# Three mixed cells of eight in an up projection, with the convolution listed piece by piece over the following cells

## The chip, the cores and the metric

One core of one Trainium2 chip runs the whole program. The metric is device time in microseconds (us), median of several executions. TensorE (PE) multiplies, VectorE (DVE) and ScalarE (ACT) work element by element, GpSimd (POOL) does a few small things, and SyncE (SP) issues most of the DMAs. ACT issues DMAs too, from a queue of its own.

## The reference

One decoder layer over 256 tokens of width 2048, all in float32: a mixer (a state-space group beside sliding-window attention), an FFN with a short convolution, and a per-layer embedding with a gate. The change lies in the FFN and the start of the embedding:

```python
h = h + jnp.concatenate([y_ssm, y_att], axis=-1) @ w_out[i]
u = _rmsnorm(h, ffn_norm_g[i]) @ w_up[i]          # 2048 -> 2 x 5632
u = _causal_dwconv(u, ffn_conv_w[i], ffn_conv_b[i])   # 3 taps along the tokens
g_ff, u_ff = jnp.split(u, [D_FF], axis=-1)
h = h + (jax.nn.silu(g_ff) * u_ff) @ w_down[i]
gate = jax.nn.sigmoid(_rmsnorm(h, ple_norm_g[i]) @ w_ple_gate[i])
pe = _rmsnorm(p[i] @ w_ple_proj[i], ple_post_g[i])
h = h + gate * pe
```

## The kernel before, in words

**Products.** Each float32 operand is split into a high and a low part (`split`, L203 to L209): ACT casts the high part (L205), DVE subtracts it from the source to get the low part (L206). A product then is three matmuls, hi x hi, hi x lo and lo x hi. Weights come in pieces of 128 x 1024 (two blocks of 128 rows by 512 columns). `load_raw` (L211) loads a piece through SP's queue into one of seven raw buffers `w`, and `split_w` (L219) makes `wh` and `wl` in one of five buffers (four in one pool, every fifth turn one in the FFN's pool). A raw buffer is free when its split is done, a split one when its matmuls are.

**The order of the work.** PE's order is the order of the program (`manual_schedule`). The other engines' rows are put in an order by a scheduler, which goes by priorities and by when it expects operands to be there. Each engine takes its instructions strictly in that order, so an instruction that waits holds up all behind it.

**The up projection.** `up(c)` (L1013) makes the gate columns and the up columns of chunk c (512 of each, 11 chunks, here called pairs) for both blocks of 128 tokens, in eight banks of PSUM. The sum over the 2048 rows goes in eight cells (`kp`) of 256 rows. A plain cell (`cell_plain`, L980) is 8 products, 24 matmuls of 128 x 512, with two weight pieces. A mixed cell (`cell_mixed`, L957) uses Strassen's scheme in Winograd's form: from sums and differences of the left side's blocks (made once, in `left`) and of the weights it takes 7 products, 21 matmuls. For that DVE makes four differences of weights, in `ta` and `tb` (L962); split are the gate piece, `ta`, `tb` and half of the up piece (`vh`, `vl`). Cells 0 and 4 are mixed. After the last of them four sums are made from the banks (L1029 to L1033), and after the last cell four more (L1035). They go to the staging tiles c0 to c3, and they set the banks free for the next pair.

**Behind a pair.** `finish` (L996) turns a half of the columns so that tokens lie along the rows: a copy (L1000), a transposing DMA from SP (L1002) and a copy into `uc` (L1003). Then `conv_tile` (L304) takes ACT's scaling with bias (L307) and two DVE steps (L309) for each of four blocks. After both halves come SiLU (L1037), the product (L1039) and the split of the product into the gated tiles `gh`, `gl`. All of that is listed at the end of `up`.

**The down projection.** The pairs are grouped in segments of 2, 2, 2, 2, 2 and 1 (L1065 to L1085). After each pair of a segment, half of the previous segment's down projection runs, in products of 12 matmuls (`down`, L1056). The first segment has none before it, so pairs 1, 2 and 3 follow each other without a down projection; the first one comes after pair 3.

**The entry.** When the mixer's output projection ends, the sum of squares of h is finished (L431, `squares` and `finish_rstd`) and its root taken. The first pair then runs its plain cells first (1, 2, 3, 5, 6, 7) and 0 and 4 last, since its left side has yet to be made. `boundary(1)` (L1042) runs, ahead of the first cell, the embedding's products `embed(0)` to `embed(3)` (L891; 12 matmuls each, whose results DVE copies to c0 to c3 (L896) and ACT's queue stores to `pe_d` (L897)), and between them `norm` and `left` for chunks 0 and 1 of h; chunks 2 and 3 follow ahead of cells 2 and 5. `norm(n)` (L901) scales 512 columns of h into `cv0` or `cv1` (n = 0 on DVE, L908; else on ACT, L906), and `left(n)` (L924) transposes them on PE (L932) and splits them with the gains, or for a mixed cell makes the seven sums and splits those. The embedding's left side `ph`, `pl` is loaded into `uc` and split (L887 to L889) when the mixer has ended.

Of the kernel before, what the change touches and what calls it, by code (L numbers as in the profile page):

```python
# [66 lines left out]
def hybrid_layer(  # L67
# [811 lines left out]
    with tc.tile_pool(name="ffn", bufs=2, reuse_waits="tile") as fp:  # L879
# [68 lines left out]
        def run(acc, lhs, rhs, start, stop):  # L948
            (hi, lo), (wh, wl) = lhs, rhs
            PE.matmul(acc, lhsT=hi, rhs=wh, start=start, stop=False)  # L950
            PE.matmul(acc, lhsT=hi, rhs=wl, start=False, stop=False)  # L951
            PE.matmul(acc, lhsT=lo, rhs=wh, start=False, stop=stop)  # L952

# [3 lines left out]
        def cell_mixed(acc, kp, c, first, last, fresh):  # L957
# [3 lines left out]
            for o, x0, x1 in ((ta[:, 0], wu[:, 0], wg[:, 0]), (ta[:, 1], wu[:, 1], wu[:, 0]), (tb[:, 0], wu[:, 1], ta[:, 0]), (tb[:, 1], wg[:, 1], tb[:, 0])):  # L961
                V.tensor_tensor(out=o, in0=x0, in1=x1, op=ALU.subtract)  # L962
# [232 lines left out]
```

## Time and profile before

| | before |
|---|---|
| median of 3 runs | 1435.52 us (1435.28 to 1436.73) |
| profiled execution | 1435.36 us, span 1433.6 us, mean granted clock 0.995 |
| PE, DVE, ACT busy | 1414.3, 1110.3, 901.6 us |
| matmul instructions | 6461 |
| entry to the FFN (last matmul of the mixer to the first of a cell) | 603.1 to 623.0 us of the span |
| pairs 1, 2, 3 | about 623 to 761 us |
| first down projection's start to 1320 | PE without a gap |

A row of a timeline gives start, duration, engine, line, the tiles (out, then in), and in brackets the idle time ahead and what ended it. A row of waits gives the total, the number and the longest. Durations of neighbouring instructions on an engine overlap a little, so the pitch from start to start is read beside them.

### The profile page before, as it was taken

The numbers are of one execution on the slowest core, as the hardware profiler recorded it, in microseconds if no ns is written. First come the engines' busy times: TensorE is split into PE (matmuls) and PEld (weight loads), VectorE is DVE, ScalarE is ACT, GpSimd is POOL, SyncE is SP. The second block draws the span as 40 slices with busy tenths as digits, with TensorE's granted clock in tenths as the row PEclk, the third lists the DMA queues.
The fourth block names the chain that finished last, engine by engine and source line by source line (L and its number), as shares of the span: only waits on it lengthen the run. The fifth ranks groups of instructions, "written<-read, shape, count | busy, mean of one in ns | idle before, by whom it ended". The sixth has DMA issues, their size and how long they took to land.

```text
span 1433.6 us, 18135 instructions
## 1 busy us (share of the span) xinstructions
PE 1414.3 (99%) x6461; PEld 1156.6 (81%) x6461; DVE 1110.3 (77%) x1480; ACT 901.6 (63%) x1196; POOL 131.5 (9%) x114
## 2 busy tenths in 40 slices
PE   9999999999999999898999999999999999999998
PEld 7888888888787778686888888888888888888887
DVE  7678876776778888688898887878788787877764
ACT  6675555644677666565787575666757576665653
POOL 0002010018344522000000000000000000000000
PEclk9999999999999999999999999999999999999999
DMA  9656655548777778565678677686766777676672
GB/s 340 232 173 207 208 184 184 162 151 231 191 208 200 205 224 227 180 229 157 191 221 219 226 213 210 217 228 199 220 216 185 239 215 214 204 222 214 219 253 67
DMA packets 164907, 296.80 MB, mean 207 GB/s; under 512 B 93201, under 2 KB 96081, under 8 KB 164177
## 3 DMA queue, kind: packets, MB, share of 16 engines
q1 hardware_dynamic: 162800, 289.94, 67.7%
q10 hardware_dynamic: 2016, 5.72, 1.1%
q8 instruction: 50, 0.82, 0.2%
q14 instruction: 41, 0.33, 0.1%
HBM read 270.41 MB, written 4.23 MB: 192 GB/s over the span
## 4 chain that ended last, share of the span: by engine, by line
PE 64%; DVE 4%; ACT 1%; issue 1%; DMA 0%; POOL 0%; DVEq 0%; ACTq 0%
PE b L951 10%; PE b L950 10%; PE b L952 10%; PE b L241 8%; PE b L243 8%; PE b L242 8%; PE acc L241 3%; PE acc L242 3%; PE acc L243 3%; DVE wl L206 2%; PE tr L802 1%; ACT wh L205 0%; PE sc L761 0%; DMA w<-in_w_up_dram 0%; PE b L293 0%
## 5 line engine op out<-in xcount | busy, mean ns | idle before, releaser
L206 DVE TENSOR_TENSOR wl<-w,wh 128x1024 fp32r<-128x1024 f32 (+1 forms) x473 | 582.7, 1240 | 208.2 <-ACT wh L205 207.3
L205 ACT CAST wh<-w 128x1024 fp32r<-128x1024 f32 (+1 forms) x473 | 488.5, 1044 | 320.5 <-PE b L952 110.7
L950 PE MATMUL b<-wh,ah 128*128 128x512 f32 x484 | 189.6, 392 | 3.9 <-DVE c L1032 2.0
L951 PE MATMUL b<-wl,ah 128*128 128x512 f32 x484 | 188.9, 390 | 0.3 <-DVE wl L206 0.3
L952 PE MATMUL b<-wh,al 128*128 128x512 f32 x484 | 189.0, 390 | 0.0
L242 PE MATMUL acc<-wl,ah 128*128 128x512 f32 x448 | 176.9, 395 | 0.0
L241 PE MATMUL acc<-wh,ah 128*128 128x512 f32 x448 | 175.8, 395 | 0.0
L243 PE MATMUL acc<-wh,al 128*128 128x512 f32 x448 | 175.6, 392 | 0.0
L241 PE MATMUL b<-wh,gh 128*128 128x512 f32 x352 | 137.1, 390 | 0.0
L243 PE MATMUL b<-wh,gl 128*128 128x512 f32 x352 | 137.0, 389 | 0.0
L242 PE MATMUL b<-wl,gh 128*128 128x512 f32 x352 | 136.9, 389 | 0.0
L950 PEld LDWEIGHTS b<-wh,ah 128*128 128x128 f32 x484 | 91.3, 189 | 24.5 <-ACT wh L205 2.4
L951 PEld LDWEIGHTS b<-wl,ah 128*128 128x128 f32 x484 | 91.2, 189 | 19.5 <-DVE wl L206 0.7
L952 PEld LDWEIGHTS b<-wh,al 128*128 128x128 f32 x484 | 91.2, 188 | 19.0
L241 PE MATMUL acc<-wh,yh 128*128 128x512 f32 x256 | 101.2, 395 | 0.3 <-DVE h L417 0.3
L242 PE MATMUL acc<-wl,yh 128*128 128x512 f32 x256 | 99.8, 390 | 0.0
L243 PE MATMUL acc<-wh,yl 128*128 128x512 f32 x256 | 99.6, 390 | 0.0
L241 PEld LDWEIGHTS acc<-wh,ah 128*128 128x128 f32 x448 | 84.2, 188 | 18.9 <-issue 1.1
L242 PEld LDWEIGHTS acc<-wl,ah 128*128 128x128 f32 x448 | 84.2, 188 | 18.4 <-issue 1.1
L243 PEld LDWEIGHTS acc<-wh,al 128*128 128x128 f32 x448 | 84.2, 188 | 17.8 <-issue 0.7
L243 PEld LDWEIGHTS b<-wh,gl 128*128 128x128 f32 x352 | 66.1, 188 | 13.7
L242 PEld LDWEIGHTS b<-wl,gh 128*128 128x128 f32 x352 | 66.1, 188 | 13.7
(289 smaller groups left out, 2256.7 us busy)
## 6 DMA issues: line engine op xcount, KB each, us to landing
w<-in_w_up_dram SPq DMA_DIRECT2D x176, 512.0 KB, 4.4
w<-in_w_in_dram SPq DMA_DIRECT2D x126, 512.0 KB, 4.1
w<-in_w_down_dram SPq DMA_DIRECT2D x88, 512.0 KB, 4.3
w<-in_w_out_dram SPq DMA_DIRECT2D x64, 512.0 KB, 4.1
w<-in_w_pg_dram SPq DMA_DIRECT2D x32, 512.0 KB, 4.4
seg<-scr SPq DMA_DIRECT2D x8, 512.0 KB, 5.0
xt<-in_xT_dram SPq DMA_DIRECT2D x16, 128.0 KB, 6.9
h<-in_x_dram SPq DMA_DIRECT2D x2, 1024.0 KB, 7.7
```

The costliest lines, as they stand in the source:

```text
L205: S.copy(hi, src)
L206: V.tensor_tensor(out=lo, in0=src, in1=hi.bitcast(F32), op=ALU.subtract)
L241: PE.matmul(acc[b], lhsT=hi, rhs=wh[:, i, :], start=(k == 0), stop=False)
L242: PE.matmul(acc[b], lhsT=hi, rhs=wl[:, i, :], start=False, stop=False)
L243: PE.matmul(acc[b], lhsT=lo, rhs=wh[:, i, :], start=False, stop=(k == total - 1 or (b == NB - 1 and k + 1 == whole)))
L802: PE.matmul(v3(o[e * HD : (e + 1) * HD, kv * 2 * P : (kv + 1) * 2 * P], 2), lhsT=v[kb][:, vs], rhs=pT[e][:, :, kb, :], start=(kb == 0), st ...
L950: PE.matmul(acc, lhsT=hi, rhs=wh, start=start, stop=False)
L951: PE.matmul(acc, lhsT=hi, rhs=wl, start=False, stop=False)
L952: PE.matmul(acc, lhsT=lo, rhs=wh, start=False, stop=stop)
```

## The change

- `MIXED` becomes (0, 3, 5). The first pair's order of cells becomes 1, 2, 0, 4, 3, 6, 5, 7, and chunks 2 and 3 of `norm` and `left` both come ahead of cell 2. The left side of plain cells 1 and 2 now lies in `ah3` and `al3`.
- The embedding's left side is loaded and split in the attention part (`at[88]`), into parts of `ah3` and `al3`, and the convolution's weights `fcw` are loaded there too. `embed` stores through SP's queue instead of ACT's. The last sum of squares, its root, and `norm` and `left` of chunks 0 and 1 get high priority.
- `cell_mixed` makes `ta` after it has listed the split of the gate piece, and `tb` after the split of `ta`.
- The convolution of a pair is cut into eight pieces, with the product and its split as a ninth. They are listed over the following work: one after each mixed cell, two after each plain one, one after each piece of a down projection, and what is left at the end of the next pair. `uc` has two buffers instead of one, and the gated tiles have three.
- `Banks` counts the products of each bank, which sets the start and stop flags of the matmuls.

```diff
-MIXED = (0, 4)
+MIXED = (0, 3, 5)
...
+        def embedding():
+            pt_ = sb(act, [P, KG, T], "ah3")[:, :KW, :]
+            nc.scalar.dma_start(pt_, pT)
+            nc.scalar.dma_start(fcw, ffn_cw)
+            t = sb(act, [P, KG, T], "al3", F32R)
+            em.extend((t[:, :KW, :], t[:, KW:, :]))
+            split(pt_, *em)
+
+        at[88] = embedding
...
-        squares(ssh, 3)
-
-    rh = finish_rstd(ssh, "rh")
+        with tc.high_priority():
+            squares(ssh, 3)
+
+    with tc.high_priority():
+        rh = finish_rstd(ssh, "rh")
...
-        pt_ = sb(fp, [P, 4, T], "uc", bufs=1)[:, :2, :]
-        nc.scalar.dma_start(pt_, pT)
-        ph, pl = (sb(fp, [P, KW, T], f"p{e}0", F32R, 1) for e in "hl")
-        split(pt_, ph, pl)
+        ph, pl = em
...
-                nc.scalar.dma_start(pe_d[b, :, n * NC : (n + 1) * NC], t)
+                nc.sync.dma_start(pe_d[b, :, n * NC : (n + 1) * NC], t)
...
-            for o, x0, x1 in ((ta[:, 0], wu[:, 0], wg[:, 0]), (ta[:, 1], wu[:, 1], wu[:, 0]), (tb[:, 0], wu[:, 1], ta[:, 0]), (tb[:, 1], wg[:, 1], tb[:, 0])):
+
+            def less(o, x0, x1):
                 V.tensor_tensor(out=o, in0=x0, in1=x1, op=ALU.subtract)
+
             g = split_w(wg)
+            less(ta[:, 0], wu[:, 0], wg[:, 0])
+            less(ta[:, 1], wu[:, 1], wu[:, 0])
             v = [sb(fp, [P, NC], f"v{e}", F32R, 1) for e in "hl"]
             split(wu[:, 1], *v)
-            a, b = split_w(ta), split_w(tb)
+            a = split_w(ta)
+            less(tb[:, 0], wu[:, 1], ta[:, 0])
+            less(tb[:, 1], wg[:, 1], tb[:, 0])
+            b = split_w(tb)
...
+        later = []
+
+        def step(n=1):
+            for _ in range(min(n, len(later))):
+                later.pop(0)()
...
+            def mult():
+                V.tensor_tensor(out=cvs[0], in0=cvs[0], in1=cvs[1], op=ALU.mult)
+                split(cvs[0], hi, lo)
+
+            later.extend([lambda e=e, f=f: conv(e, f) for e in range(2) for f in range(4)] + [mult])
...
-                kps.sort(key=lambda kp: kp in MIXED)
+                kps = plain[:-len(MIXED)]
+                for m, p in zip(MIXED, plain[-len(MIXED):]):
+                    kps += [m, p]
...
+                step(1 if kp in MIXED else 2)
+            step(len(later))
             for t, m in ((c0, Q2), (x, Q4), (y, Q3), (z, Q22)):
                 V.tensor_tensor(out=t, in0=t, in1=acc[m], op=ALU.add)
-            cg = finish(c, (c0, x))
-            S.activation(out=cg, in_=cg, func=AF.Silu)
-            cu = finish(NPAIR + c, (y, z))
-            V.tensor_tensor(out=cg, in0=cg, in1=cu, op=ALU.mult)
-            return cg
+            gated(c, (c0, x), (y, z), hi, lo)
...
-            if kp == 1:
+            if kp == plain[0]:
+                with tc.high_priority():
+                    norm(0)
                 for n in range(3):
                     embed(n)
-                norm(0)
-                left(0)
-                norm(1)
+                with tc.high_priority():
+                    left(0)
+                    norm(1)
                 embed(3)
-                left(1)
-            elif kp in (2, 5):
-                n = 2 + kp // 5
-                norm(n)
-                left(n)
+                with tc.high_priority():
+                    left(1)
+            for n in range(2, KG):
+                if kp == plain[min(n, len(plain) - len(MIXED)) - 1]:
+                    norm(n)
+                    left(n)
...
-                gemm(acc, lhs, [w_down[i, n] for i in range(i0 * KG // KW, (i0 + ni) * KG // KW)])
+                for s in range(total):
+                    products(acc, lhs, load_w(w_down[i0 * KG // KW + s, n]), s * KW, KW, total * KW, s == total - 1)
+                    step()
```

The order of the rows on an engine shows what is moved. Before, on DVE at the entry, from the last two weight splits of the mixer's time to the first copies of the embedding (`s1` and `rs_t` belong to the root, `cv0` is the first normed chunk, `c0` and `c1` hold embeddings, `pl0` is the low part of the embedding's left side):

```order
L206 TENSOR_TENSOR wl_1160_5536<-w_1158_5533,wh_1159_5535 128x1024
L206 TENSOR_TENSOR wl_1169_5580<-w_1167_5577,wh_1168_5579 128x1024
L431 TENSOR_REDUCE s1_1105_5373<-ssh_507_2637 128x2
L206 TENSOR_TENSOR pl0_1116_5408<-uc_1114_5405,ph0_1115_5407 128x512
L198 TENSOR_SCALAR rs_t_1106_5375<-s1_1105_5373 128x2
L908 TENSOR_SCALAR cv0_1147_5498<-h0_1_83,rh_1107_5377 128x512
L908 TENSOR_SCALAR cv0_1147_5498<-h1_2_84,rh_1107_5377 128x512
L896 COPY c0_1131_5440<-b_1126_5420 128x512
L896 COPY c1_1132_5443<-b_1127_5421 128x512
```

Now, right behind the same two splits (`ta`, `tb`, `vl` and their `w` belong to the first mixed cell):

```order
L997 TENSOR_TENSOR ta_1193_5705<-w_1192_5703,w_1191_5701 128x512
L997 TENSOR_TENSOR ta_1193_5705<-w_1192_5703 128x512
L918 COPY c0_1128_5435<-b_1123_5415 128x512
L432 TENSOR_REDUCE s1_1108_5380<-ssh_508_2638 128x2
L207 TENSOR_TENSOR vl_1198_5714<-w_1192_5703,vh_1197_5713 128x512
L918 COPY c1_1129_5438<-b_1124_5416 128x512
L997 TENSOR_TENSOR tb_1194_5706<-w_1192_5703,ta_1193_5705 128x512
L207 TENSOR_TENSOR wl_1169_5595<-w_1167_5592,wh_1168_5594 128x1024
L918 COPY c2_1135_5461<-b_1130_5441 128x512
L199 TENSOR_SCALAR rs_t_1109_5382<-s1_1108_5380 128x2
L918 COPY c3_1136_5464<-b_1131_5442 128x512
L997 TENSOR_TENSOR tb_1194_5706<-w_1191_5701,tb_1194_5706 128x512
```

and then:

```order
L207 TENSOR_TENSOR wl_1187_5668<-w_1185_5665,wh_1186_5667 128x1024
L918 COPY c0_1142_5487<-b_1137_5467 128x512
L918 COPY c1_1143_5490<-b_1138_5468 128x512
L930 TENSOR_SCALAR cv0_1122_5412<-h0_1_83,rh_1110_5384 128x512
L930 TENSOR_SCALAR cv0_1122_5412<-h1_2_84,rh_1110_5384 128x512
```

The subtractions and the half split of mixed cell 0, all copies of the first three embeddings and two weight splits now stand ahead of `cv0`; the split of `pl0` is gone from here.

Before, on DVE from the first pair to the second (`c0` to `c3` take the sums out of the banks, `ta` and `tb` belong to the second pair's first mixed cell from the second `ta` on):

```order
L206 TENSOR_TENSOR wl_1275_6036<-tb_1267_6018,wh_1274_6035 128x1024
L1031 TENSOR_TENSOR c1_1241_5941<-c2_1242_5942,b_1121_5415 128x512
L1035 TENSOR_TENSOR c0_1240_5940<-c0_1240_5940,b_1122_5416 128x512
L206 TENSOR_TENSOR wl_1278_6063<-w_1276_6060,wh_1277_6062 128x1024
L206 TENSOR_TENSOR wl_1281_6081<-w_1279_6078,wh_1280_6080 128x1024
L1032 TENSOR_TENSOR c2_1242_5942<-c2_1242_5942,b_1120_5414 128x512
L1035 TENSOR_TENSOR c1_1241_5941<-c1_1241_5941,b_1124_5418 128x512
L206 TENSOR_TENSOR wl_1287_6117<-w_1285_6114,wh_1286_6116 128x1024
L1033 TENSOR_TENSOR c3_1243_5943<-c2_1242_5942,b_1121_5415 128x512
L962 TENSOR_TENSOR ta_1296_6172<-w_1295_6170,w_1294_6168 128x512
L962 TENSOR_TENSOR ta_1296_6172<-w_1295_6170 128x512
L1035 TENSOR_TENSOR c2_1242_5942<-c2_1242_5942,b_1123_5417 128x512
```

Now, at the same place:

```order
L1085 TENSOR_TENSOR c2_1241_5916<-c0_1239_5914,b_1115_5405 128x512
L207 TENSOR_TENSOR wl_1278_6012<-ta_1271_5999,wh_1277_6011 128x1024
L1086 TENSOR_TENSOR c1_1240_5915<-c2_1241_5916,b_1117_5407 128x512
L207 TENSOR_TENSOR wl_1280_6018<-tb_1272_6000,wh_1279_6017 128x1024
L1092 TENSOR_TENSOR c0_1239_5914<-c0_1239_5914,b_1118_5408 128x512
L997 TENSOR_TENSOR ta_1297_6136<-w_1296_6134,w_1295_6132 128x512
L997 TENSOR_TENSOR ta_1297_6136<-w_1296_6134 128x512
L1087 TENSOR_TENSOR c2_1241_5916<-c2_1241_5916,b_1116_5406 128x512
L207 TENSOR_TENSOR wl_1284_6049<-w_1282_6046,wh_1283_6048 128x1024
L1092 TENSOR_TENSOR c1_1240_5915<-c1_1240_5915,b_1120_5410 128x512
L997 TENSOR_TENSOR tb_1298_6137<-w_1296_6134,ta_1297_6136 128x512
L1088 TENSOR_TENSOR c3_1242_5917<-c2_1241_5916,b_1117_5407 128x512
```

Sums of the banks, splits of the first pair's last mixed cell and subtractions of the second pair's first one are interleaved. Before, the first pair ended with a mixed cell as well.

In a later pair, on DVE at its first mixed cell, before (`cv0` and `cv1` take the convolution of the pair ahead, `h0` and `h1` the down projection's sums):

```order
L309 SCALAR_TENSOR_TENSOR cv0_1649_7808<-uc_1644_7797,fcw_1108_5389,cv0_1649_7808 128x254
L206 TENSOR_TENSOR wl_1697_8020<-w_1692_8009,wh_1696_8019 128x1024
L206 TENSOR_TENSOR wl_1701_8028<-ta_1694_8013,wh_1700_8027 128x1024
L206 TENSOR_TENSOR wl_1703_8032<-tb_1695_8014,wh_1702_8031 128x1024
L309 SCALAR_TENSOR_TENSOR cv1_1655_7833<-uc_1650_7822,fcw_1108_5389,cv1_1655_7833 128x255 x2
L417 TENSOR_TENSOR h0_1_83<-h0_1_83,b_1670_7925 128x512
L309 SCALAR_TENSOR_TENSOR cv1_1655_7833<-uc_1650_7822,fcw_1108_5389,cv1_1655_7833 128x255
L309 SCALAR_TENSOR_TENSOR cv1_1655_7833<-uc_1650_7822,fcw_1108_5389,cv1_1655_7833 128x254
L309 SCALAR_TENSOR_TENSOR cv1_1655_7833<-uc_1650_7822,fcw_1108_5389,cv1_1655_7833 128x255
L309 SCALAR_TENSOR_TENSOR cv1_1655_7833<-uc_1650_7822,fcw_1108_5389,cv1_1655_7833 128x254
L417 TENSOR_TENSOR h1_2_84<-h1_2_84,b_1671_7926 128x512
```

Now:

```order
L310 SCALAR_TENSOR_TENSOR cv0_1808_8441<-uc_1793_8399,fcw_18_144,cv0_1808_8441 128x254
L207 TENSOR_TENSOR wl_1848_8617<-w_1843_8610,wh_1847_8616 128x1024
L207 TENSOR_TENSOR wl_1852_8627<-ta_1845_8614,wh_1851_8626 128x1024
L310 SCALAR_TENSOR_TENSOR cv1_1823_8531<-uc_1798_8410,fcw_18_144,cv1_1823_8531 128x255 x4
L997 TENSOR_TENSOR ta_1869_8736<-w_1868_8734,w_1867_8732 128x512
L997 TENSOR_TENSOR ta_1869_8736<-w_1868_8734 128x512
L310 SCALAR_TENSOR_TENSOR cv1_1823_8531<-uc_1798_8410,fcw_18_144,cv1_1823_8531 128x254 x3
L207 TENSOR_TENSOR wl_1854_8633<-tb_1846_8615,wh_1853_8632 128x1024
L310 SCALAR_TENSOR_TENSOR cv1_1823_8531<-uc_1798_8410,fcw_18_144,cv1_1823_8531 128x254
L207 TENSOR_TENSOR wl_1857_8663<-w_1855_8660,wh_1856_8662 128x1024
```

The split of `tb` stood right behind that of `ta`. Seven steps of the convolution and the next mixed cell's two subtractions have moved between them.

More of the change, by code (lines that the diff above doesn't have):

```diff
@@ L193, in hybrid_layer @@
     posi = sb(const, [P, NB], "posi", I32)
+    fcw = sb(const, [P, 88 * 4], "fcw")
     fill(mc)
@@ L946, in left, with __init__, __getitem__, run @@
                 left_parts[kp] = hi, lo
[L948 to L952, printed above, removed]
         P1, P6, P7, P5, Q2, Q4, Q3, Q22 = range(8)
         A11, A12, A22, S1, S2, S3, S4 = range(7)
-        def cell_mixed(acc, kp, c, first, last, fresh):
+        class Banks:
+            def __init__(self):
+                self.t = [bank() for _ in range(8)]
+                self.left = [len(MIXED)] * 4 + [len(MIXED) + KW * len(plain)] * 3 + [KW * len(plain)]
+                self.used = set()
+            def __getitem__(self, m):
+                return self.t[m]
+            def run(self, m, lhs, rhs):
+                (hi, lo), (wh, wl) = lhs, rhs
+                self.left[m] -= 1
+                PE.matmul(self.t[m], lhsT=hi, rhs=wh, start=m not in self.used, stop=False)
+                PE.matmul(self.t[m], lhsT=hi, rhs=wl, start=False, stop=False)
+                PE.matmul(self.t[m], lhsT=lo, rhs=wh, start=False, stop=not self.left[m])
+                self.used.add(m)
+        def cell_mixed(acc, kp, c):
             wg, wu = (load_raw(w_up[n, kp]) for n in (c, NPAIR + c))
             ta, tb = (sb(fp, [P, KW, NC], t, bufs=1) for t in ("ta", "tb"))
-            for o, x0, x1 in ((ta[:, 0], wu[:, 0], wg[:, 0]), (ta[:, 1], wu[:, 1], wu[:, 0]), (tb[:, 0], wu[:, 1], ta[:, 0]), (tb[:, 1], wg[:, 1], tb[:, 0])):
+            def less(o, x0, x1):
                 V.tensor_tensor(out=o, in0=x0, in1=x1, op=ALU.subtract)
             g = split_w(wg)
+            less(ta[:, 0], wu[:, 0], wg[:, 0])
+            less(ta[:, 1], wu[:, 1], wu[:, 0])
             v = [sb(fp, [P, NC], f"v{e}", F32R, 1) for e in "hl"]
             split(wu[:, 1], *v)
-            a, b = split_w(ta), split_w(tb)
+            a = split_w(ta)
+            less(tb[:, 0], wu[:, 1], ta[:, 0])
+            less(tb[:, 1], wg[:, 1], tb[:, 0])
+            b = split_w(tb)
             right = {P1: (g, 0), Q2: (g, 1), P5: (a, 0), P7: (a, 1), P6: (b, 0), Q4: (b, 1)}
@@ L969, in cell_mixed @@
             left_ = {P1: A11, Q2: A12, Q3: S4, P5: S1, P7: S3, P6: S2, Q4: A22}
-            order = (P1, P5, P7, P6, Q4, Q2, Q3) if first and fresh else (P1, Q2, Q3, P5, P7, P6, Q4)
+            order = (P1, Q2, Q3, P5, P7, P6, Q4) if acc.used else (P1, P5, P7, P6, Q4, Q2, Q3)
             for m in order:
@@ L977, in cell_mixed, with cell_plain @@
                     r = [t[:, i, :] for t in w]
-                run(acc[m], (hi[:, f, :], lo[:, f, :]), r, first and (fresh or m in (P1, P5, P6, P7)), last and (m in (P1, P5, P6, P7) or not fresh))
-        def cell_plain(acc, kp, c, first, last, fresh):
+                acc.run(m, (hi[:, f, :], lo[:, f, :]), r)
+        def cell_plain(acc, kp, c):
             h, l = left_parts[kp]
@@ L987, in cell_plain, with turned @@
                         bs = slice(b * P, (b + 1) * P)
-                        run(
-                            acc[m],
-                            (h[:, i, bs], l[:, i, bs]),
-                            [t[:, i, :] for t in w],
-                            first and (not fresh or m == Q22) and i == 0,
-                            last and (fresh or m == Q22) and i == KW - 1,
-                        )
-        def finish(c, us):
-            uc = sb(fp, [P, 4, T], "uc", bufs=1)
+                        acc.run(m, (h[:, i, bs], l[:, i, bs]), [t[:, i, :] for t in w])
+        later = []
+        def step(n=1):
+            for _ in range(min(n, len(later))):
+                later.pop(0)()
+        def turned(us):
+            uc = sb(fp, [P, 4, T], "uc")
             for b in range(NB):
@@ L1077, in hybrid_layer @@
             pair += np_
+        step(len(later))
         h2T = Lhs(act, KT, "a")
```

55 lines of the change are left out of this document (32 added, 23 removed).

## Prediction

> **What bounds the kernel now.** I read the page first, for the busy shares:
>
> ```profile
> span 1433.6 us, 18135 instructions
> PE 1414.3 (99%) x6461; PEld 1156.6 (81%) x6461; DVE 1110.3 (77%) x1480; ACT 901.6 (63%) x1196; POOL 131.5 (9%) x114
> ```
>
> TensorE (PE) has work 99% of the span, so what counts is the number of its matmuls, and the few places where it waits. Next came the view of PE's waits (line, releaser; total us, times, longest), of which these four lie in the part that the change touches:
>
> ```profile
> PE b L241 <- ACT ph L205: 4.1, 1, 4.1
> PE b L950 <- DVE c L1035: 2.8, 2, 1.4
> PE b L950 <- DVE c L1032: 2.0, 1, 2.0
> PE b L950 <- DVE c L1033: 0.5, 1, 0.5
> ```
>
> PE's timeline puts the first at the entry to the FFN: the last matmul of the mixer's output projection, the embedding's first and last half-speed ones, the transposes of the first normed chunk (called T(0) below), and the first up-projection matmul. The last five rows are the end of the first pair and the start of the second:
>
> ```profile
> 603.10 0.39 PE L243 MATMUL acc<-wh,yl 128*128 128x512 f32 x1
> 607.60 0.79 PE L241 MATMUL b<-wh,ph 128*128 128x512 f32 x1 [4.11 <-ACT ph L205]
> 612.15 0.63 PE L242 MATMUL b<-wl,ph 128*128 128x512 f32 x1
> 612.58 0.63 PE L243 MATMUL b<-wh,pl 128*128 128x512 f32 x1
> 618.58 1.04 PE L932 MATMUL b<-ident,cv 128*128 128x128 f32 x8
> 619.38 0.47 PE L241 MATMUL b<-wh,ph 128*128 128x512 f32 x1
> 623.02 0.48 PE L950 MATMUL b<-wh,ah 128*128 128x512 f32 x1
> 670.37 0.50 PE L950 MATMUL b<-wh,ah 128*128 128x512 f32 x1 [1.38 <-DVE c L1035]
> 673.33 0.47 PE L950 MATMUL b<-wh,ah 128*128 128x512 f32 x1 [1.98 <-DVE c L1032]
> 675.56 0.79 PE L950 MATMUL b<-wh,ah 128*128 128x512 f32 x1 [0.48 <-DVE c L1033]
> 678.65 0.80 PE L950 MATMUL b<-vh,ah 128*128 128x512 f32 x1 [1.44 <-DVE c L1035]
> 681.38 0.46 PE L950 MATMUL b<-wh,ah 128*128 128x512 f32 x1
> ```
>
> From 612.15 to 612.58 is 0.43 us for one matmul; elsewhere the pitch is about half of that. The windows give the pitch and the granted clock by stage (us, busy and count of each engine, clock, DMA):
>
> ```profile
> 603.50:623.00 19.50, 15.40 (x64) 12.38 (x65) 14.12 (x23) 11.35 (x19) 0.71 (x1) 0.82 0.69 217
> 667.50:682.00 14.50, 9.12 (x26) 5.54 (x26) 13.30 (x18) 9.92 (x11) 0.00 (x0) 0.76 0.89 237
> 641.20:761.10 119.90, 114.20 (x489) 92.21 (x488) 103.54 (x137) 84.56 (x99) 0.00 (x0) 0.97 0.68 200
> 846.80:889.10 42.30, 42.30 (x189) 35.02 (x188) 35.33 (x42) 23.07 (x25) 0.00 (x0) 1.00 0.67 211
> 724.50:1320.00 595.50, 595.50 (x2629) 493.23 (x2628) 487.69 (x619) 393.89 (x444) 0.00 (x0) 1.00 0.73 216
> ```
>
> The stretch from 846.80 is the up projection of one later pair: two mixed cells of 21 matmuls and six plain ones of 24, 186 (three of the 189 overlap the edges), in 42.30 us: 0.2275 us a matmul. From 724.5 on PE is busy in every microsecond and VectorE (DVE) in 487.69 of 595.50, 82%. So the steady part is bound by matmuls alone, and before it lie two losses. The entry: from 603.5 to 607.6 PE idles, and about 12 matmuls then run at 0.43, 7.0 us in all (4.1, and 12 x 0.20, and the slow first one). The first transitions: from 641.2 to 761.1 lie 486 matmuls, 110.6 us at 0.2275, in 119.9, so 9.4 us are lost, nearly all between 667.5 and 682, where DVE is busy 13.30 of 14.50.
>
> **The change part by part.** The sum is made against the profiled execution, 1435.36 us with a span of 1433.6; the median of the runs shown is 1435.52, 0.01% above it.
>
> *Matmuls.* A third mixed cell in each of 11 pairs takes away 24 - 21 = 3 matmuls: 33 x 0.2275 = **-7.5 us**. They lie in stretches where PE is never idle, so all of it counts unless DVE takes it back.
>
> The Trainium skill ("TensorE: Matmul & The Clock Gate", "Wait — 56ns, not 53.3ns?") states 215.7 ns from start to start for 512 columns at the warm clock; by that the term would be 7.1. The trace has 227.5, and the sum goes by it.
>
> *DVE's price.* By form, count, busy us and mean ns of one:
>
> ```profile
> L206 DVE TENSOR_TENSOR wl<-w,wh 128x1024 fp32r<-128x1024 f32 x467 | 578.6, 1247 | 205.7 <-ACT wh L205 204.8
> L962 DVE TENSOR_TENSOR tb<-w,ta 128x512 f32<-128x512 f32 x22 | 15.0, 684 | 0.0
> L206 DVE TENSOR_TENSOR vl<-w,vh 128x512 fp32r<-128x512 f32 x22 | 15.0, 684 | 0.0
> L309 DVE SCALAR_TENSOR_TENSOR cv<-uc,fcw,cv 128x254 f32<-128x254 f32 x88 | 40.8, 477 | 0.0
> L1035 DVE TENSOR_TENSOR c<-c,b 128x512 f32<-128x512 f32 x44 | 28.8, 680 | 0.0
> ```
>
> Back to back they overlap by some 0.08 us, as DVE's timeline shows at the second transition:
>
> ```profile
> 704.54 0.68 DVE L1030 TENSOR_TENSOR c<-c,b 128x512 f32<-128x512 f32 x1
> 705.14 1.22 DVE L206 TENSOR_TENSOR wl<-w,wh 128x1024 fp32r<-128x1024 f32 x1
> 706.28 0.68 DVE L962 TENSOR_TENSOR ta<-w,w 128x512 f32<-128x512 f32 x1
> ```
>
> So 0.60 for 512 columns, 1.13 for 1024, and 0.40 for a convolution step. A mixed cell costs DVE four subtractions, one half split and three whole ones: 5 x 0.60 + 3 x 1.13 = 6.4. A plain cell costs two splits, 2.26. A pair besides has eight sums out of the banks (4.8), 16 convolution steps (6.4), the product and its split (2.3): 13.5. That makes 2 x 6.4 + 6 x 2.26 + 13.5 = 39.8 per pair before, and 3 x 6.4 + 5 x 2.26 + 13.5 = 43.9 after. PE takes 42.3 before and 183 x 0.2275 = 41.6 after.
>
> *Steady pairs.* Eight pairs have a down projection with each up: 96 matmuls more for PE (21.8 us), eight splits and four additions for DVE (11.4). DVE then needs 55.4 of 63.5 us, 87%. Taken at **0**, covered by the weight buffers (four, and one more): PE holds up to five halves of a cell, 2.7 us each. Without that cover it costs rival B's price.
>
> *Entry.* The embedding's left side is loaded and split in the attention part, at slot 88, so the wait of 4.11 goes: embed(0) to (2) can start at 603.6 and their 36 matmuls end at 611.8. The cast and subtraction, 0.6 us each, move to where ACT and DVE have slack: nothing, at most 1 us. But T(0) needs the normed chunk cv0 from DVE. In the trace, before T(0), stand:
>
> ```profile
> 603.03 1.28 DVE L417 TENSOR_TENSOR h<-h,acc 128x512 f32<-128x512 f32 x2
> 605.49 2.36 DVE L206 TENSOR_TENSOR wl<-w,wh 128x1024 fp32r<-128x1024 f32 x2 [1.19 <-ACT wh L205]
> 609.42 0.89 DVE L908 TENSOR_SCALAR cv<-h,rh 128x512 f32<-128x512 f32 x2 [0.82 <-POOL rh L200]
> ```
>
> In the new order 15 rows stand between those two splits and the first cv0: four subtractions of the first mixed cell, its half split, six copies of embeddings (11 x 0.60), two whole splits (2.3), two small ones (0.2): 9.1 us. The splits end at about 606.6, though the mixed cell's weights, issued when a split at 603 has freed their buffer, may land up to a microsecond later:
>
> ```profile
> w<-in_w_up_dram SPq DMA_DIRECT2D x176, 512.0 KB, 4.4
> pe_d<-c ACTq DMA_DIRECT2D x8, 256.0 KB, 4.6
> ```
>
> cv0's first half is then ready at 616.2 to 617.1; I take T(0) at 616.4. PE has idled 4.6 us by then and, as after the 4.11 us at 607.6, runs at half speed for 5.4 us: T(0) 1.6, nine matmuls of embed(3) 3.8, three at full speed 0.7, T(1) 0.8, so the first plain cell starts at 623.3 instead of 623.02. Its low part lies in al3, which embed(3) reads until 622.5; behind that DVE has two copies, a split of 896 columns, a whole one and three pieces of gains, 4.5 us, up to the one that the cell's sixth matmul needs, at 626.8 where PE is there at 624.4. So 0.3 + 2.4 = **+2.7** against before (-4 if cv0 came in time, +5 if more of the queue is late).
>
> The same page ("Part 1: The HAM clock gate") states that the clock is halved after an idle window of about 3.4 us. The rows at 607.60 and after agree. By it the waits of 2 us below would cost no clock; but the rows at 675.56 and 678.65 are slow (0.63 to 0.80) after waits of 1.38, 1.98 and 0.48.
>
> *Stores of the embedding* go to SP's queue. Behind them wait weight loads, and the copies into c0 to c3 wait for the store two embeddings earlier. The first is issued at about 608.4 and lands by the 4.6 us above at 613.0, where the copy that needs it comes up at about 614.5: nothing, up to +1. ACT saves eight issues, which nothing waited for. fcw's earlier load, the third buffer of gated tiles and the second uc are priced at nothing, since no row names them as a releaser of PE.
>
> *Transitions without a down projection.* Pairs 2 and 3 follow without one, and there DVE needs 43.9 against PE's 41.6: a deficit of 2.3 each, 4.6 in all. DVE's own waits come on top (this row shows one):
>
> ```profile
> 676.71 0.69 DVE L962 TENSOR_TENSOR ta<-w,w 128x512 f32<-128x512 f32 x1 [1.20 <-DMA w<-in_w_up_dram]
> ```
>
> Two of these and some tenths: 2.7. With 1.0 for matmuls at half speed (five at 0.20) that is 8.3 instead of 9.4: **-1.1**. The mixed cell's splits in order of use help the first products of a cell; the convolution in pieces only spreads what DVE does.
>
> Sum: -7.5 + 2.7 + 0 - 1.1 = -5.9, so 1435.36 - 5.9 = **1429.5 us**.
>
> **The rivals.** *A, the stalls go as well.* If cv0 is in time (a subtraction that waits for its load being all that is late) and the spread convolution lets PE run through both transitions, the losses of 7.0 and 9.4 go with the matmuls: -23.9, 1411.5. For it: before, DVE was held up at 667.5 by convolution and bank sums in one lump, and ph was a plain mistake of order. Against: DVE's sums above, and 15 rows before cv0. Half of it gives 1418.
>
> *B, slower: the first mixed cell of each steady pair.* There the split of tb now stands behind seven convolution steps and two subtractions (2.8 + 1.2) and takes 1.1 itself, 5.1 us, while PE has six matmuls (1.4 us) between the first use of ta and that of tb. If DVE is less than 3.7 us ahead there, PE waits; 2.4 ahead costs 1.3 per pair, eight times: +10.4, in all -5.9 + 10.4 = +4.5, 1439.9. Against: five buffers let DVE run 5 to 8 us ahead, and in 595.5 us before PE never waited.
>
> *C, no change.* Entry and transitions eat it: a cold clock at both transitions, 12.0 us instead of 8.3, and 5 instead of 2.7 at the entry: 1429.5 + 3.7 + 2.3 = 1435.5. For it: the row of 13.30 busy of 14.50, where a third mixed cell leaves DVE no slack.
>
> That the change doesn't take place is excluded: PE's order has 33 rows fewer.
>
> **How the numbers follow.** The forecast has 0.55, A 0.17, B 0.10, C 0.15, the rest 0.03. A measurement of this kernel can tell about 0.2%, 2.9 us, from no change; the bounds are 1432.6 and 1438.4. The forecast's own spread (entry -4 to +5, transitions 2 either way) is 1424 to 1434. Faster: A, most of the forecast: 0.74. Within: C and the forecast's upper end: 0.16. Slower: 0.10. The range leaves out B and the lower half of A: 1416 to 1437.
>
> **What would show it.** Right: PE counts 33 fewer; a wait at T(0) of 4 to 5 us on cv from DVE where 4.11 on ph stood, then matmuls at 0.43; waits for DVE's sums (L1085 to L1092) or splits (L207) of some 8 us in the two transitions; none from about 720 on, and the steady up at 41.6. Wrong: T(0) without a wait (A), waits of L986's rows on wl from tb in each steady pair (B), or an up that isn't 0.7 us shorter.

## The result, and the profile after

The changed kernel takes 1445.03 us (median of 6 runs, 1440.78 to 1446.83), before 1436.45 (6 runs): ratio 1.0057, 95% interval 1.0041 to 1.0072. It is slower, where 1429.5 was forecast. The profiled execution took 1441.96 us (span 1440.2), 6.6 more than that of before, and is the second fastest of its six: the other 3 us up to the median have no profile, and what follows explains the 6.6.

PE's waits after:

```profile
PE b L954 <- DVE cv L930: 5.6, 1, 5.6
PE b L987 <- DVE wl L207: 4.8, 7, 1.4
PE b L986 <- DVE c L1092: 4.6, 3, 2.5
PE sc L762 <- POOL qT L713: 2.8, 2, 1.7
PE acc L242 <- DVE nm L774: 1.7, 1, 1.7
PE b L988 <- DVE al L210: 1.2, 1, 1.2
```

The wait for ph is gone, and one for cv0 stands in its place. The second row grew from one wait of 0.3 us before to seven. The fourth and fifth lie in the mixer, whose only term in the prediction, the moved cast and subtraction, was taken at nothing. The windows by stage, first of before (pairs 1 to 3, then the eight steady pairs), then of after (entry, pairs 1 to 3, steady pairs, and two single ups):

```profile
623.00:761.00 138.00, 132.30 (x577) 107.38 (x576) 119.77 (x163) 97.22 (x118) 0.00 (x0) 0.98 0.67 201
761.00:1272.40 511.40, 511.40 (x2258) 423.57 (x2257) 419.29 (x529) 335.37 (x377) 0.00 (x0) 1.00 0.72 214
```

```profile
607.60:627.40 19.80, 14.25 (x66) 11.62 (x64) 16.96 (x28) 11.19 (x18) 0.71 (x1) 0.91 0.83 271
627.40:765.70 138.30, 131.66 (x567) 106.29 (x566) 127.39 (x176) 100.55 (x123) 0.00 (x0) 0.98 0.61 189
765.70:1278.50 512.80, 508.79 (x2233) 418.10 (x2232) 453.77 (x580) 349.82 (x394) 0.00 (x0) 1.00 0.75 215
787.50:830.70 43.20, 41.80 (x185) 34.29 (x184) 39.10 (x46) 25.20 (x27) 0.00 (x0) 1.00 0.65 204
1044.80:1086.30 41.50, 41.50 (x185) 34.36 (x184) 37.37 (x42) 23.79 (x25) 0.00 (x0) 1.00 0.70 215
```

| stage | before | after | difference | forecast |
|---|---|---|---|---|
| up to the mixer's end | 603.5 | 607.6 | +4.1 | 0 |
| entry | 19.5 | 19.8 | +0.3 | +0.3 |
| pairs 1 to 3 | 138.0 | 138.3 | +0.3 | -0.7 (9 matmuls fewer -2.0, al3 +2.4, transitions -1.1) |
| eight steady pairs | 511.4 | 512.8 | +1.4 | -5.5 (24 matmuls fewer) |
| the rest | | | +0.5 | 0 |

Two of the eight ups of the steady pairs run in 41.5 us, as forecast; the others take 41.9 to 43.2, and what the eight have above 41.5 is 6.9 us in all. The first has most. The chain of waits there (start, us, what; `...` marks rows left out) shows why:

```profile
766.27 5.43 DMA flip<-half
...
772.80 0.99 ACT half L1041
...
776.85 5.29 DMA flip<-half
...
783.24 1.06 ACT wh L206
784.32 1.23 DVE wl L207
785.55 1.19 DVE cv L310 x3
786.73 1.20 DVE ta L997 x2
787.93 1.24 DVE cv L310 x4
789.18 0.25 issue
789.43 0.68 DVE h L418
790.11 1.15 DVE wl L207
791.30 0.50 PE b L987
```

Read upward from the last row: PE waits for the split of tb (790.11), which DVE reaches after a convolution of seven steps, two subtractions and a sum for h. All of these stand behind the split of ta (784.32), and that waits for ACT's cast of ta (783.24). On ACT the cast stands behind the copies of the turned columns, and those wait for two transposing DMAs of over 5 us, one after the other. PE's row says what it costs:

```profile
791.30 0.50 PE L987 MATMUL b<-wl,ah 128*128 128x512 f32 x1 [1.40 <-DVE wl L207]
```

PE's waits from 765.7 to 1278.5, all steady pairs together:

```profile
PE b L987 <- DVE wl L207: 4.0, 5, 1.4
```

The rest of the 6.9 are for the most part matmuls at and near such places that start 0.32 to 0.40 us apart instead of 0.23. Three of the five waits (1.40, 0.17 and 0.80) stand at the split of tb, as in the chain. The two others (0.82 and 0.79) come 11 to 12 us into their up, at the first split of its third cell, a plain one; first DVE's row, then PE's:

```profile
925.75 2.35 DVE L207 TENSOR_TENSOR wl<-w,wh 128x1024 fp32r<-128x1024 f32 x2
```

```profile
928.15 0.50 PE L987 MATMUL b<-wl,ah 128*128 128x512 f32 x1 [0.82 <-DVE wl L207]
```

DVE has had no idle time there since the split of ta at 912.16, 16 us earlier: its lead is used up.

### The profile page after: what moved, and what is told of

Its sections match the earlier page's. It is cut to its first block, busy times and chain, and to the rows that moved or that the text cites. A ratio compares the mean times of both kernels' runs of the same rounds, so it can differ in the third digit from the quotient of the medians.

```text
span 1440.2 us, 18164 instructions
## 1 busy us (share of the span) xinstructions
PE 1412.0 (98%) x6428; PEld 1149.4 (80%) x6428; DVE 1161.8 (81%) x1549; ACT 920.3 (64%) x1219; POOL 127.9 (9%) x113
## 4 chain that ended last, share of the span: by engine, by line
PE 46%; DVE 10%; DMA 6%; ACT 4%; issue 4%; DVEq 0%; ACTq 0%; SPq 0%
PE b L987 8%; PE b L988 8%; PE b L986 8%; DVE wl L207 5%; PE b L243 5%; PE b L244 5%; PE b L242 5%; DMA flip<-half 4%; PE acc L242 3%; PE acc L243 3%; PE acc L244 3%; DVE cv L310 2%; ACT wh L206 2%; DMA w<-in_w_up_dram 2%; ACT half L1041 1%
## 5 line engine op out<-in xcount | busy, mean ns | idle before, releaser
L207 DVE TENSOR_TENSOR wl<-w,wh 128x1024 fp32r<-128x1024 f32 (+1 forms) x462 | 576.1, 1255 | 187.6 <-ACT wh L206 186.8
L206 ACT CAST wh<-w 128x1024 fp32r<-128x1024 f32 (+1 forms) x462 | 477.3, 1044 | 318.0 <-PE b L988 118.4
L987 PE MATMUL b<-wl,ah 128*128 128x512 f32 x374 | 147.2, 394 | 4.0 <-DVE wl L207 4.0
L986 PE MATMUL b<-wh,ah 128*128 128x512 f32 x374 | 147.1, 393 | 0.9 <-DVE c L1092 0.8
L988 PE MATMUL b<-wh,al 128*128 128x512 f32 x374 | 146.6, 392 | 1.2 <-DVE al L210 1.2
L987 PE MATMUL b<-wl,ph 128*128 128x512 f32 x264 | 103.0, 390 | 0.8 <-DVE wl L207 0.8
L988 PE MATMUL b<-wh,pl 128*128 128x512 f32 x264 | 102.8, 389 | 0.0
L986 PE MATMUL b<-wh,ph 128*128 128x512 f32 x264 | 102.7, 389 | 0.0
L987 PEld LDWEIGHTS b<-wl,ah 128*128 128x128 f32 x374 | 70.8, 189 | 20.9 <-DVE wl L207 6.3
L986 PEld LDWEIGHTS b<-wh,ah 128*128 128x128 f32 x374 | 70.8, 189 | 16.8 <-DVE c L1092 1.2
```

Of the source, the lines that this page charges most:

```text
L206: S.copy(hi, src)
L207: V.tensor_tensor(out=lo, in0=src, in1=hi.bitcast(F32), op=ALU.subtract)
L986: PE.matmul(self.t[m], lhsT=hi, rhs=wh, start=m not in self.used, stop=False)
L987: PE.matmul(self.t[m], lhsT=hi, rhs=wl, start=False, stop=False)
L988: PE.matmul(self.t[m], lhsT=lo, rhs=wh, start=False, stop=not self.left[m])
```

## Experiments

Each ratio is to the kernel before, run beside it on the same chip. "Stretch" is the time from the mixer's end to the first down projection (entry and pairs 1 to 3): 157.5 before, 158.1 after. "Steady" is from there over eight pairs: 511.4 and 512.8. Both come from one profile of each run.

**Which part of the change loses?** e1 puts the third mixed cell alone into the kernel before, e2 takes it out of the changed one.

```diff
-MIXED = (0, 4)               # e1, in the kernel before (boundary: cells 2 and 6)
+MIXED = (0, 3, 5)
-MIXED = (0, 3, 5)            # e2, in the changed kernel
+MIXED = (0, 4)
```

> The kernel before with MIXED = (0, 3, 5) alone (with three pairs of gated tiles, so that it fits; one buffer for uc; the embedding at the entry; the first pair's mixed cells last). 33 matmuls fewer, as after. If the steady loss of 6.9 us comes from where the convolution's second half stands (two buffers for uc), the steady ups run at 41.6 us and the time is 1430 to 1434. If a third mixed cell is more than DVE can do in a steady pair, wherever the convolution stands, the ups take 42 to 43 us as after, and the time is 1437 or more. The mixer's end is at 603.5 in either case if its 4.1 us come from the embedding's earlier load and split.

> The changed kernel with MIXED = (0, 4): everything but the third mixed cell. 33 matmuls more than after. If DVE's load is the cause, the steady ups run at 42.3 us without a wait, and what is left is the mixer's 4.1 and the entry: 1437 to 1440. If the place of the convolution is enough to make PE wait, there are waits on wl in the first mixed cell of the steady pairs here too, 3 us or more in all, and the time is 1441 or more.

e1: 1446.87 us, ratio 1.0071 (1.0059 to 1.0083); stretch 169.3, steady 510.2, mixer's end 603.2. e2: 1428.62 us, ratio 0.9938 (0.9922 to 0.9955); stretch 145.3, steady 517.3, mixer's end 607.3. So by the medians the third mixed cell loses some 16 us where the rest is in place, and 10 alone; the rest of the change gains 8. e2's windows (entry, pairs 1 to 3, steady pairs):

```profile
607.30:619.70 12.40, 12.40 (x64) 10.38 (x64) 10.19 (x17) 8.89 (x15) 1.61 (x1) 1.00 0.78 269
619.70:752.60 132.90, 129.95 (x578) 106.13 (x576) 120.86 (x166) 96.94 (x118) 0.00 (x0) 1.00 0.71 210
752.60:1269.90 517.30, 514.17 (x2258) 424.50 (x2257) 421.29 (x531) 338.24 (x378) 0.00 (x0) 1.00 0.73 213
```

The entry has no idle time at all, 7.1 us less than before, and pairs 1 to 3 are 5.1 shorter with the same matmuls. My bound for e2 was missed on the good side. But its steady pairs take 5.9 us more than before, also with the same matmuls; the first up alone takes 46.2 instead of 42.2. On DVE seven steps of the convolution stand between the splits of ta and tb there too:

```profile
773.75 1.23 DVE L207 TENSOR_TENSOR wl<-ta,wh 128x1024 fp32r<-128x1024 f32 x1 [1.12 <-ACT wh L206]
774.89 2.84 DVE L310 SCALAR_TENSOR_TENSOR cv<-uc,fcw,cv 128x255 f32<-128x255 f32 x7
777.66 1.22 DVE L207 TENSOR_TENSOR wl<-tb,wh 128x1024 fp32r<-128x1024 f32 x1
```

So a steady loss doesn't need the third mixed cell; and by e1 it doesn't need the second buffer of uc either, since e1's 510.2 are 4.3 above the 511.4 - 5.5 that its matmuls leave. The two profiles differ by 9.2 us, not by 16: e2's is the slowest of its six runs, that of after the second fastest. Against e2, after loses 7.4 at the entry and 5.4 in pairs 1 to 3, and is 4.5 shorter in the steady pairs.

**Is it the second uc buffer, or the embedding's place?**

```diff
-            uc = sb(fp, [P, 4, T], "uc")            # e3; the same in left
+            uc = sb(fp, [P, 4, T], "uc", bufs=1)
```

e4 restores the loading and splitting of ph and pl at the entry, into uc and tiles of their own. e6 and e7 are e3's and e4's edits with two mixed cells.

> The changed kernel with one buffer for uc, as before. On DVE the split of tb then stands two rows behind that of ta and not nine. If the place of the convolution is the cause of the steady loss, 5 to 7 us go: the profiled time falls to 1435 to 1437. If DVE's load is the cause, the loss moves to another cell and the time stays within 2 us of after.

> The changed kernel with the embedding's left side loaded and split at the entry, into uc and tiles of its own, as before. If its earlier place costs the mixer its 4.1 us, the mixer ends at 603.5 again, and PE then waits about 4 us for ph instead of 5.6 us for cv0: 3 to 5 us off. If the 4.1 us are the run's own (DMA and waits on GpSimd), the mixer ends at 607 as after.

> The changed kernel with MIXED = (0, 4) and one buffer for uc. With two mixed cells and two buffers, pairs 1 to 3 took 132.9 us against 138.0 before. If the second buffer brought that, they take 136 to 138 here and the time is 1432 or more; if the first pair's order of cells (a plain cell last) brought it, they stay at 132 to 134 and the time within 2 us of 1428.6.

> The changed kernel with MIXED = (0, 4) and the embedding's left side loaded and split at the entry as before. The wait for ph of 4 us returns with about 3 us of half-speed matmuls: the entry takes 18 to 20 us and not 12.4; of the mixer's 4 us some 2 go: 1432 to 1435. If the early embedding is only a change of place, 1427 to 1430.

e3: 1444.43, ratio 1.0051 (1.0039 to 1.0063), steady 512.3. The seven steps no longer stand between the two splits, and the loss stays; as the second half of its forecast said, it has moved to another cell: all the waits of the steady pairs now stand at splits of plain cells, and the first up runs in 41.5. With three mixed cells the place of the convolution isn't the cause by itself. e4: 1444.92, ratio 1.0062 (1.0042 to 1.0083); mixer's end 605.4, between the two bounds, and entry 23.4: what the mixer gives back, waits for ph (4.8) and pl (3.0) take. e6: 1430.79, ratio 0.9949 (0.9932 to 0.9966); pairs 1 to 3 take 136.2 against e2's 132.9, so the second buffer helps there by 3 us. In the steady pairs it costs more than that: e6 runs them without a wait, as before, where e2 took 517.3.

```profile
753.50:1264.90 511.40, 511.40 (x2258) 423.45 (x2257) 421.29 (x532) 337.23 (x378) 0.00 (x0) 1.00 0.73 215
```

The medians don't tell e2 and e6 apart; e6's profile is the fastest of its six runs. But e7 and e16 (below), with two mixed cells and two buffers as e2, take 513.3 and 513.6 there, with seven and four steps between the two splits: the sign holds, and the size scatters.

e7: 1433.56, ratio 0.9979 (0.9965 to 0.9993); entry 18.9 against 12.4, as forecast. With two mixed cells the early embedding is what gains at the entry.

**Is the steady loss DVE's load?** e5 leaves out the two DVE steps of the FFN's convolution, e12 the transposing DMA (uc is copied from columns that aren't turned), e13 both. e10 computes all, with tb's subtractions on GpSimd.

```diff
-        for s in range(1, n):                       # e5, e13, in conv_tile
+        for s in range(1, n if n != 3 else 1):
-                nc.sync.dma_start_transpose(flip, half)        # e12, e13
+                flip = half.rearrange("p (c t) -> p c t", c=8)
-            less(tb[:, 0], wu[:, 1], ta[:, 0])      # e10; the second one too
+            G.tensor_tensor(out=tb[:, 0], in0=wu[:, 1], in1=ta[:, 0], op=ALU.subtract)
```

> The changed kernel with the two DVE steps of the FFN's convolution left out (one tap of three is computed): 16 x 0.40 = 6.4 us less for DVE in a pair, 43.9 becomes 37.5, below the 39.8 of before; matmuls, loads and ACT's work are those of after. If DVE's load is the cause, the waits of pairs 1 to 3 fall by 8 us or more and the steady ups run at 41.5: 1427 to 1432. If the third mixed cell costs by something else (its loads, ACT's casts, the banks), the time stays within 4 us of after, 1441 or more.

> The changed kernel without the transposing DMA: the columns are copied to uc without being turned (the result is that of other data). SP issues 44 transfers fewer, and ACT doesn't wait for them ahead of the casts of ta and tb. If that latency is what holds pairs 1 to 3 with a third mixed cell, the stretch from the mixer's end to the first down projection falls from 158.1 to 150 or less. If it is not on the path, it stays at 156 or more; the steady ups stay at 42 to 43 in either case, since DVE's work is the same.

> The changed kernel without the transposing DMA and without the two DVE steps of the convolution. If latency of the turned columns and DVE's load together are the cause, that stretch falls to 145 or less and the steady ups run at 41.5: 1418 to 1424. If the raw weight loads and the splits of three mixed cells alone hold it, it stays above 152 and the time above 1428.

> The changed kernel with the two subtractions of tb on GpSimd instead of DVE: 2 x 0.60 x 3 = 3.6 us less for DVE in a pair, 40.3 instead of 43.9, near the 39.8 of before; nothing is left out. If DVE's time is what the steady ups wait for, they run at 41.5 to 42 us instead of 42.3, and the time falls by 3 to 7 us. If GpSimd's subtraction takes so long, or slows DVE so much, that tb comes late, the waits on tb's split grow and the time is that of after or more.

e5: 1437.14, ratio 0.9999 (0.9988 to 1.0010). e12: 1433.69, ratio 0.9983 (0.9974 to 0.9992). e13: 1436.26, ratio 1.0000 (0.9992 to 1.0009). Their steady stages, first e5's (e13's has the same 505.90), then e12's:

```profile
765.90:1271.80 505.90, 505.90 (x2234) 418.90 (x2233) 407.14 (x449) 348.45 (x393) 0.00 (x0) 1.00 0.73 216
```

```profile
761.80:1269.20 507.40, 506.53 (x2234) 418.75 (x2233) 456.36 (x581) 350.16 (x394) 0.00 (x0) 1.00 0.63 201
```

505.90 is the forecast's 511.4 - 5.5: without the convolution's DVE steps PE never waits in a steady pair, and the 24 matmuls that these pairs save are worth what was priced. Without the transposing DMA all but 1.5 us go too, with DVE's work the same (456 us busy); the waits at tb's split are gone, and of those at the third cell two are left (0.32 and 0.55). So the wait at tb's split in after needs both DVE's queue of some 5 us and a lead that the turned columns have used up; the later waits are DVE's queue, with the transposing DMA or without it. e12's expectation that the steady ups wouldn't change was wrong, and its stretch, 155.4, lies between the two bounds that were set. In pairs 1 to 3 e5 and e13 missed their forecasts: their stretches are 161.5 and 162.8, longer than after's 158.1, so their times stay near 1437.

e10: 1444.49, ratio 1.0052 (1.0037 to 1.0067). The steady ups after the first run at 41.5 to 42.0, but the first takes 45.4, the eight steady pairs 511.1, and pairs 1 to 3 take 142.3. GpSimd's rows, and DVE's splits over the steady pairs, first of after, then of e10:

```profile
L1006 POOL TENSOR_TENSOR tb<-w,tb 128x512 f32<-128x512 f32 x33 | 116.0, 3516 | 2.6
L1005 POOL TENSOR_TENSOR tb<-w,ta 128x512 f32<-128x512 f32 x33 | 63.6, 1927 | 507.0 <-DVE ta L997 294.2 <-DVE wl L207 197.3 <-ACT wh L206 15.4
```

```profile
L207 DVE TENSOR_TENSOR wl<-w,wh 128x1024 fp32r<-128x1024 f32 x187 | 227.2, 1219 | 54.6 <-ACT wh L206 54.5
```

```profile
L207 DVE TENSOR_TENSOR wl<-w,wh 128x1024 fp32r<-128x1024 f32 x189 | 253.2, 1358 | 38.9 <-ACT wh L206 38.4
```

**Does the first pair's order of cells cost the entry, and is that the loss?** e9 puts a third plain cell ahead of the first mixed one, e11 adds e10's edit. e8 has two mixed cells in pairs 1 to 3 and three from pair 4 on, with one uc buffer.

```diff
-                kps = plain[:-len(MIXED)]           # e9, e11
-                for m, p in zip(MIXED, plain[-len(MIXED):]):
-                    kps += [m, p]
+                kps = [1, 2, 4, 0, 3, 6, 5, 7]
+            mixed = MIXED if c >= 3 else (0, 5)     # e8, in up
```

> The changed kernel, three mixed cells, with one edit: the first pair's order of cells is 1, 2, 4, 0, 3, 6, 5, 7 (a third plain cell ahead of the first mixed one). On DVE no subtraction of a mixed cell then stands ahead of cv0. If those rows are why PE waits 5.6 us at the entry, the entry falls from 19.7 to 12 to 14 us and the time to 1436 to 1439. If cv0 waits for something else (the sum of squares, GpSimd's root), the entry stays at 19 or more and the time at 1442 or more.

> Both edits: the first pair's order of cells 1, 2, 4, 0, 3, 6, 5, 7, and tb's subtractions on GpSimd. If both reasons hold and add up, the entry is 12 to 14 us, the steady ups 41.5 to 42, and the time 1426 to 1432, at or below that of two mixed cells (1428.6). If only one of them holds, 1434 to 1440.

> Two mixed cells (0 and 5) in pairs 1 to 3 and a third (3) from pair 4 on, with one buffer for uc; cell 3's left side is made in both forms. 24 matmuls fewer than before. If the loss of after lies in the entry and pairs 1 to 3, where there is no down projection, this runs at 1424 to 1429. If the steady pairs lose as much as the third mixed cell saves, it is no better than two mixed cells everywhere, 1428 to 1432; if they lose more, 1433 or more.

e9: 1441.61, ratio 1.0033 (1.0018 to 1.0048). The entry is 12.4, as expected; the time is above the 1436 to 1439 expected with it. DVE's row there, and the window of pairs 1 to 3:

```profile
612.50 0.88 DVE L930 TENSOR_SCALAR cv<-h,rh 128x512 f32<-128x512 f32 x2
```

```profile
618.70:766.10 147.40, 135.27 (x568) 107.84 (x567) 132.84 (x184) 103.19 (x126) 0.00 (x0) 0.95 0.62 191
```

cv0 is ready 7 us after the mixer's end at 606.3, where it took 14 in after; yet pairs 1 to 3 take 147.4 us, 9 more than after. In this profile, the second slowest of its twelve runs and 3 us above their median, the next stage takes what the entry gives, so the wait at the entry alone didn't set the stretch's end. e11: 1448.03, ratio 1.0081 (1.0061 to 1.0101): the two don't add up, they clash. Its stretch is 170.1, in a profile 5 us above the median. e8: 1434.55, ratio 0.9981 (0.9967 to 0.9994): entry 12.4, pairs 1 to 3 143.9 (cell 3's left side is made twice there), steady 509.3. Of 24 matmuls (5.5 us) the steady pairs keep 2; what makes it slower than e2 lies in pairs 1 to 3, not where its forecast had put that.

**The raw buffers, and the listing.**

```diff
-WR = 7                       # e14, three mixed cells; e16, two
+WR = 6
```

> The changed kernel with six raw weight buffers instead of seven. If the raw loads are on the path (a mixed cell holds two buffers until tb is made), the stretch from the mixer's end to the first down projection grows by 5 us or more and the steady ups by some tenths: 1450 or more. If there is room in the seven, the time stays within 2 us of after.

> The changed kernel with MIXED = (0, 4) and six raw weight buffers. With three mixed cells six buffers took 6.7 us off the entry, since the subtractions then stood behind cv0; with two they stand behind it anyway. So no gain is expected: 1427 to 1433. If the seventh buffer costs by itself (loads that land too early and press on the others), 1424 or less.

> The changed kernel with four edits undone in the listing: the convolution listed in one piece at the end of its pair, all subtractions of a mixed cell ahead of its splits, no high priority, the embedding's left side listed after the mixer. The order of the rows on every engine is that of after, row by row. So nothing can change but by what the runs themselves scatter: 1441 to 1447. A time outside that would mean that something other than the order decides.

e14 was expected to lose and gains: 1436.89, ratio 1.0008 (0.9998 to 1.0017), 7 us better than after by the two ratios. With six buffers the order on DVE has cv0 ahead of most of the mixed cell's work (entry 13.0), and the stretch is 154.1; the steady pairs stay at 512.1. e16: 1431.29, ratio 0.9971 (0.9960 to 0.9982): no gain over e2. e15 undoes four edits of the listing at once and has after's order on every engine: 1445.28, ratio 1.0071 (1.0052 to 1.0090), as after. So the convolution in pieces, the splits in order of use, the high priority and the slot of the embedding change nothing that runs: it was the second uc buffer, not the listing in pieces, that moved the seven steps between the two splits. Left are the set of mixed cells, the first pair's order of cells, the tiles and buffers, and the queue of the stores; no run tried that queue by itself. e15's steady pairs take 510.7 where after's take 512.8, with the same rows in the same order, so such a number scatters by some 2 us from run to run.

Of all these, e2 has the lowest median, below both before and after; e6 is not clearly behind it.

## Why the prediction was wrong

The profiled execution lies 12.5 us above the forecast: 6.9 in the steady pairs, 4.1 in the mixer, 1.0 in pairs 1 to 3 and 0.5 behind them.

- **Matmuls, -7.5: right as a price.** 33 fewer; e5's steady stage keeps every one of the 24 in it. The other nine lie in pairs 1 to 3, where PE does wait, and no run shows them apart.
- **Steady pairs, "taken at 0, covered by the weight buffers": the step that failed.** It measured 512.8 - 505.9 = 6.9 us. The place and the mechanism are rival B's, its price 10.4. The working there put DVE 5 to 8 us ahead; in the chain above the split of ta ends at 785.55, and PE, which starts the up at 787.47, reads it at 788.38. That is 2.8 ahead. In between DVE has 5.7 us (the sum for h came on top of 5.1) against PE's 1.4: 4.3 - 2.8 = 1.5, near the 1.40 of the row. The 87% of DVE were right (453.77 of 512.80 is 88%), but a mean share doesn't say how far ahead an engine is at its densest place, and I took the lead from the number of buffers without ACT, whose casts stood behind columns still in flight. e12 and e5 show both halves at this place. B wasn't right either: it had this wait in all eight pairs, where three have it, and the two waits in a third cell were in nobody's sum.
- **The second uc, "priced at nothing": wrong too, in the same place.** The reason given was that no row named it. e2, e7 and e16 against e6 show that it moves steps of the convolution between the two splits and costs 2 to 6 us in the steady pairs with two mixed cells; with three (after against e3) the loss is there with either number of buffers.
- **Mixer, "nothing, at most 1 us": +4.1, the second miss.** Some of DVE's rows stand elsewhere in the attention part. PE's wait for nm of 1.7 is new there, and that for qT grew by 0.6. In before and in e1, whose rows there stand as in before, the mixer ends at 603.5 and 603.2; in after, e2 and e15 at 607.6, 607.3 and 606.7. The wait for nm (1.5 to 2.2) is in every kernel with the embedding loaded in the attention part and in none of the four without (before, e1, e4, e7), so that much belongs to the move. The rest is open: e4 and e7, without the move, end at 605.4 and 604.6, the others with it anywhere from 603.8 to 610.5, and the wait for qT scatters from 0.7 to 2.9.
- **Entry, +2.7: right in kind, 1.6 in size** (0.3, and 1.3 of waits in the first cell). DVE's and PE's rows of after:

```profile
611.80 0.69 DVE L997 TENSOR_TENSOR ta<-w,w 128x512 f32<-128x512 f32 x1 [1.07 <-DMA w<-in_w_up_dram]
620.82 0.87 DVE L930 TENSOR_SCALAR cv<-h,rh 128x512 f32<-128x512 f32 x2
```

```profile
621.35 2.15 PE L954 MATMUL b<-ident,cv 128*128 128x128 f32 x8 [5.55 <-DVE cv L930]
623.72 0.63 PE L243 MATMUL b<-wl,al 128*128 128x512 f32 x1
624.15 0.52 PE L244 MATMUL b<-wh,al 128*128 128x512 f32 x1
624.50 0.39 PE L242 MATMUL b<-wh,al 128*128 128x512 f32 x1
```

  From the first subtraction to cv0 lie 9.0 us, where 9.1 were added up; the load came 1.07 late, so T(0) waited 5.55 and not 4.6. The half speed lasted 2.8 us and not the 5.4 that I took from the other wait. e9, with those rows behind cv0, has neither. That the clock drops after an idle window of about 3.4 us is what the Trainium skill says ("TensorE: Matmul & The Clock Gate", "Part 1: The HAM clock gate"), and the rows agree: 0.43 us from 623.72 to 624.15, behind 5.55 us idle.
- **Transitions, -1.1: wrong by some 2 us, and in its reason.** The stage came out at +0.3; with 2.0 for the matmuls and 1.3 of al3's waits that leaves +1.0 for them. I worked them out as DVE's deficit of 2.3 a pair. e5 takes 6.4 from DVE in each, DVE is then busy for 117.93 of 141.70 us in pairs 1 to 3, and the stretch is 161.5, no shorter. So a full DVE isn't what holds them there. What does stays open: e12 (155.4), e13 (162.8) and e14 (154.1) don't fall into one line, and every edit moves the order too.
- **Chances.** The forecast's own case held the steady pairs free of waits, and B had 0.10. Faster was given 0.74, though A's 0.17 and all of the forecast's 0.55 come to 0.72 and a part of that belonged to no change. Two things spoke for B and were in hand: the order showed the nine rows between the splits, and DVE's share was to rise from 82 to 87%.

## What to carry to other kernels

A cheaper form of a product that asks more of the vector engine pays only where that engine's lead, at its densest place, covers its queue: work out there when the operand is ready and when it is read, with every engine that stands ahead in the chain, rather than share against share. Where a scheduler sets the order, an edit of the listing may do nothing and a number of buffers much: read the new order before pricing either. And take such a bundle apart: here one part lost 16 us and the others gained 8.
